# Half-products in both ConvGLUs of a two-layer decoder step, and one fixed place per feature tile for the modulation's matmuls

## The chip, the core and the metric

The kernel runs on one core of one Trainium2 chip, in one launch. The metric is the device time of the run in microseconds (us). Matmuls run on TensorE (PE; its weight loads are PEld), elementwise work on VectorE (DVE), ScalarE (ACT) and GpSimd (POOL); loads are issued by SyncE (SP), one queue, in order.

## What is computed

The program is one inference step of a two-layer decoder over 1024 prompt tokens and 8 sample tokens (1032 together, D_MODEL 1024, D_FF 2816). Layer 0 mixes tokens with a gated MLP, layer 1 with sparse attention; after each comes a ConvGLU:

```python
def ada_params(c, w_ada, b_ada):
    return (jax.nn.silu(c) @ w_ada + b_ada).reshape(c.shape[0], N_MOD, D_MODEL)

def conv_glu(h, w_up, conv_w, conv_b, w_down, past):
    a, u = jnp.split(h @ w_up, 2, axis=-1)
    t = a.shape[1]
    full = jnp.concatenate([past, a], axis=1)
    conv = sum(full[:, j:j + t] * conv_w[j] for j in range(CONV_W)) + conv_b
    y = (jax.nn.gelu(conv) * u) @ w_down
    return y, full[:, -(CONV_W - 1):]
```

`ada_params` gives the scales, shifts and gates (the modulation) of each layer. Those of layer 1 depend on `c` alone, so they can be computed at any time before layer 1.

## The kernel before

Everything lies with features on the partitions and tokens along the free axis. Float32 operands are split into a high and a low part, and each product is three matmuls: high by high, high by low, low by high (`mm3`, L97 is the one line of all such matmuls). Tokens come in chunks of 384, 384 and 264.

`conv_glu(l, ...)` walks over 22 feature tiles of 128. An **ordinary tile** (`parts`, `dense`) computes the gate and the up projection: 2 projections x 3 chunks x 8 blocks of the contraction x 3 = 144 matmuls into the four PSUM banks psA. Then it convolves, applies gelu and multiplies (DVE, ACT), and splits the result into `gh` and `gl`. The **down projection** of a tile (`down`) is 24 pieces of 3 matmuls into the four banks psB, each added to the residual R by DVE (`accumulate`, L649 and L653); these 72 matmuls wait in a queue `dq` and are dealt out between the matmuls of the next tile (`dpump`).

In the second ConvGLU only (`SEVEN = (1,)`) the tiles 4 to 21 are made by `seven_tile`. It takes gate and up weights as two halves of the contraction each (A11, A12 of the gate, A21, A22 of up) and the first 688 tokens as two chunks of 344 (`TH`), and forms that 2 x 2 block product from seven half-products, with sums of weights (S1 to S4, made by `sums` on POOL) and sums of inputs (F, made once by `form_steps` on DVE, ACT and POOL during tiles 2 and 3). The last 344 tokens take four plain half-products. A half-product is 12 matmuls of 344 columns (L840), so a tile has 11 x 12 = 132 of them. Each weight operand goes through `operand`: ACT makes the high half, POOL the low half (`ws`). The matmuls of these tiles are pinned in program order; in all other places a scheduler decides the order on each engine.

Raw weights land in three buffers (`raws`, `rawmk`), shared by gate and up weights (`wraw`, or `load_w` in an ordinary tile), down weights (`load_rows`, L137), the input sums and the modulation's weights.

**The modulation's steps** (`ada_round`). Layer 1's modulation is three rounds of eight steps and an end (`fin`: copy, four transposes, additions), 27 items in the deque `slow`, worked off inside the first ConvGLU. A step loads two raw buffers of 512 KB and issues four matmuls of 512 columns (L258), each into its own 32 partitions of one psB bank that a round holds from its first step to its end. The function `background` is called after each of the six parts of a tile and takes an item at every fourth call:

```python
            if slow and not fq and tick[0] % 4 == 0:
                slow.popleft()()
```

Of the kernel before, what the change touches and what calls it, by code (L numbers as in the profile page):

```python
# [17 lines left out]
KT = 8  # L18
# [29 lines left out]

KEEP = (3, 3)

SEVEN = (1,)
TH = 344
S0 = 4

# [7 lines left out]
def hybrid_step(  # L62
# [7 lines left out]
    V, A, G, PE, SP = nc.vector, nc.scalar, nc.gpsimd, nc.tensor, nc.sync  # L70
# [15 lines left out]
    def bank(tag="A"):  # L86
        return psum.tile([128, 512], F32, name="ps" + tag, tag="ps" + tag)
# [3 lines left out]
    def pinned(i):  # L91

        if pin[0]:
            tc.keep_in_program_order(i)
# [63 lines left out]
    fq = deque()  # L158
# [45 lines left out]
    SCT = sm.tile([128, KT, 32], F32, name="SCT", tag="x1")  # L204
    V.memset(SCT, 0.0)
    b = bank("B")
# [39 lines left out]
    def ada_round(L, r, mk):  # L246

        st = {}

        def step(k):  # L250
            if k == 0:
                st["b"] = bank("B")
            rw = [mk(), mk()]
            for half in range(2):
                SP.dma_start(rw[half][:, :1024],
                             w_ada[L, k * 128:(k + 1) * 128, 2048 * r + 1024 * half:2048 * r + 1024 * half + 1024])
            for g in range(4):
                PE.matmul(st["b"][32 * g:32 * g + 32, :512], SCT[:, k, :], rw[g // 2][:, (g % 2) * 512:(g % 2 + 1) * 512],  # L258
                          start=(k == 0), stop=(k == KT - 1), skip_group_check=True)

        def fin():
            S = mk()
            A.activation(S[:, :512], st["b"], AF.Copy)
            b2 = bank("B")
            for j in range(4):
                tr(b2[:, j * 128:(j + 1) * 128], S[:, j * 128:(j + 1) * 128])
            bb = PAR[:, pBADA + L * 48 + 16 * r:pBADA + L * 48 + 16 * r + 16].rearrange("p (g j) -> p g j", j=4)
            mo = MOD[L][:, 16 * r:16 * r + 16, :].rearrange("p (g j) c -> p g j c", j=4)
            src = b2.rearrange("p (j g c) -> p g j c", j=4, g=4)
            for g in range(4):  # L270
                V.tensor_tensor(mo[:, g], src[:, g, :, 0:9], bb[:, g].unsqueeze(2).to_broadcast([128, 4, 9]), op=OP.add)

        out = [lambda k=k: step(k) for k in range(KT)]
        out.append(fin)
        return out

    def rawmk():
# [169 lines left out]
    b = bank("B")  # L447
# [103 lines left out]
    b = bank("B")  # L551
    left = deque(range(KT))
    for n, (i, c) in enumerate((i, c) for c in range(3) for i in range(2)):
        z_half(i, c, 0)
        for _ in range(1 if n < 4 else 2):
            k = left.popleft()
# [61 lines left out]
    for i in range(8, 16):  # L618
        m = i - 8
        U[m] = Tt("U", tag="PPTT"[m % 4])  # L620
        for c in range(3):
            b = dense(pieces[i], 128, c)
# [46 lines left out]
    def conv_glu(l, R, gate, tail_af, last, slow, prefetch=None):  # L669
        up = ffn_w_up[l]  # L670
        keep = KEEP[l]

        seven = l in SEVEN

# [31 lines left out]
        def dpump(n):  # L706
            for _ in range(n):
                if dq:
                    dq.popleft()()

        tick = [0]

        def background():
            pump(2)
            tick[0] += 1
            if slow and not fq and tick[0] % 4 == 0:
                slow.popleft()()

        class Tile:
# [83 lines left out]
        def wraw(ff, s):  # L803
            if ff < FT:
                t = raws.tile([128, SLOT], F32, name="raw", tag="raw")
                SP.dma_start(t[:, :1024].rearrange("p (k c) -> p k c", k=KT),
                             up[:, s * F + ff * 128:s * F + (ff + 1) * 128].rearrange("(k p) c -> p k c", p=128))
                raw_w[ff, s] = [t[:, 0:512], t[:, 512:1024]]
# [27 lines left out]
        def half_product(b, w, xs, first, last=True):  # L836
            for k in range(4):
                x = [x[k] for x in xs]
                for n, (i, j) in enumerate(((0, 0), (0, 1), (1, 0))):
                    pinned(PE.matmul(b[:, :TH], w[i][:, k, :], x[j], start=first and k == 0 and n == 0, stop=last and k == 3 and n == 2,  # L840
                                     skip_group_check=True))

        def seven_tile(ff):
# [8 lines left out]
            def x(i, j):  # L852
                return [[H[:, 4 * i + k, j * TH:(j + 1) * TH] for k in range(4)] for H in (Hh, Hl)]
# [4 lines left out]
            def W(name):  # L858
                return ops[ff, name]
# [13 lines left out]

            def step(n):
                dpump(n)
                background()


            ba = bank("A")
# [10 lines left out]
            A.activation(p5, bb[:, :TH], AF.Copy)  # L890
            step(DP[2])
            operand(ff, "S4")
            wraw(ff + 1, 0)

            bd = bank("A")
            half_product(bd, W("S2"), t(1), True)
# [7 lines left out]
            conv(0, TH, ba, 0)  # L904
            gelu(a)
            step(DP[4])
            half_product(be, W("A12"), x(1, 2), False)
            A.activation(Cc[:, 2 * TH:NPT], be[:, :nr], AF.Identity, scale=w2, bias=cb)
            V.scalar_tensor_tensor(Cc[:, NPT:T], be[:, nr:TH], w2, PSC[l][:, ff, :], op0=OP.mult, op1=OP.add)
# [83 lines left out]
        if seven:  # L993
            operand(S0, "A11")
            sums(S0, 1)
            operand(S0, "S1")
            operand(S0, "S2")
            operand(S0, "A12")
            sums(S0, 3)
            dpump(len(dq) - 24)  # L1000
            pin[0] = True
            for ff in range(S0, FT):
                seven_tile(ff)
            pin[0] = False
# [15 lines left out]
        b = bank("B")  # L1020
# [11 lines left out]
    slow = deque(x for r in range(3) for x in ada_round(1, r, rawmk))  # L1032
# [61 lines left out]
    b = bank("B")  # L1094
# [323 lines left out]
    for w in range(2):  # L1418
        kf = [Tt("kf0", tag="P"), Tt("kf1", tag="P")]
        for kvh in range(2):  # L1420
# [4 lines left out]
            for c in range(3):  # L1425
                b = dense(pcs[i], 128, c)
# [334 lines left out]
```

## Time and profile before

| | |
|---|---|
| median of 3 runs | 2605.18 us (2605.16 to 2605.95) |
| the profiled execution's own time | 2597.94 us |
| its span, from the first instruction to the last | 2596.2 us |
| granted TensorE clock over the span | 0.985 |

| engine | busy us | share of the span |
|---|---|---|
| PE | 2495.1 | 96% |
| PEld | 2332.8 | 90% |
| DVE | 1679.4 | 65% |
| POOL | 1193.8 | 46% |
| ACT | 890.7 | 34% |

How to read it: the profile is one execution, and its times are us from the start of the span. A matmul's duration in a row reaches from its start to its modelled end and overlaps the next one; what a matmul costs PE in a stream is the distance from its start to the next start. The granted clock is given as a share of full speed. In the chain that ended last, a piece "PE x24" is 24 matmuls with nothing between them.

### The profile page before, as it was taken

To read this page: it belongs to the slowest core of one execution; us is meant where nothing else is said; L and a number is where in the kernel's file an instruction comes from. 1 tells how busy PE (TensorE), PEld (TensorE's weight loads), DVE (VectorE), ACT (ScalarE), POOL (GpSimd) and SP (SyncE) were. 2 spreads that over 40 slices of the span, in tenths; PEclk is the share of its full clock that TensorE was granted. 3 is DMA by queue.
4 is the path that set the end of the run, shared out by engine and by line. 5 is a ranking of instruction groups with operands and counts; after the bars stand their busy time and mean duration, and the time that the engine had idled before them with its cause. 6 is when DMAs were issued, how large, how long until landed. Compare 5 with 4: busy or idle time off the path is not lost.

```text
span 2596.2 us, 40912 instructions
## 1 busy us (share of the span) xinstructions
PE 2495.1 (96%) x15768; PEld 2332.8 (90%) x15768; DVE 1679.4 (65%) x3761; ACT 890.7 (34%) x1763; POOL 1193.8 (46%) x1236
## 2 busy tenths in 40 slices
PE   7999999999999999999998989898999999999996
PEld 5898899999999999998987988877999999999996
DVE  5233335667666666655687996533698788778777
ACT  4121234111111111113566876542523333333341
POOL 3332535223222322334435666533645666666665
PEclk9999999999999999999999999999999999999998
DMA  8414302322222223111113111133211111111111
GB/s 277 131 53 124 105 17 76 95 89 66 90 84 72 90 66 98 58 38 51 61 35 106 50 54 61 46 119 114 74 50 35 52 53 50 49 49 49 50 49 76
DMA packets 203977, 192.14 MB, mean 74 GB/s; under 512 B 9806, under 2 KB 178246, under 8 KB 202999
## 3 DMA queue, kind: packets, MB, share of 16 engines
q1 hardware_dynamic: 200582, 179.86, 22.2%
q0 software_dynamic: 2688, 9.44, 1.1%
q8 instruction: 125, 2.05, 0.3%
q14 instruction: 69, 0.57, 0.1%
q10 hardware_dynamic: 513, 0.23, 0.0%
HBM read 178.41 MB, written 11.27 MB: 73 GB/s over the span
## 4 chain that ended last, share of the span: by engine, by line
PE 83%; DVE 8%; POOL 3%; issue 2%; DMA 2%; ACT 2%; POOLq 0%; SPq 0%; DVEq 0%; ACTq 0%
PE psA L97 36%; PE psB L97 25%; PE psA L840 14%; PE psB L198 3%; PE psB L258 3%; DVE junk L1215 1%; DVE S L1195 1%; PE psA L198 1%; ACT junk L1246 1%; POOL whi L116 1%; DMA raw<-in_dsa_w_out_dram 0%; ACT Hh L384 0%; DMA adaw<-in_w_ada_dram 0%; DVE wh L119 0%; PE psA L1574 0%
## 5 line engine op out<-in xcount | busy, mean ns | idle before, releaser
L649 DVE SCALAR_TENSOR_TENSOR R<-psB,g,R 128x384 f32<-128x384 f32 (+1 forms) x976 | 537.0, 568 | 310.5 <-PE psB L97 308.1
L97 PE MATMUL psA<-Hh,whi 128*128 128x384 f32 (+1 forms) x2032 | 657.0, 324 | 12.5 <-POOL whi L116 7.9
L97 PE MATMUL psA<-Hl,whi 128*128 128x384 f32 (+1 forms) x2032 | 652.2, 322 | 1.0 <-POOL Hl L390 0.9
L97 PE MATMUL psA<-Hh,wlo 128*128 128x384 f32 (+1 forms) x2032 | 651.6, 321 | 1.4 <-DVE wlo L119 0.7
L116 POOL TENSOR_SCALAR whi<-raw 128x1024 fp32r<-128x1024 f32 (+1 forms) x125 | 137.3, 1098 | 653.6 <-PE psA L97 498.6
L97 PEld LDWEIGHTS psA<-Hh,whi 128*128 128x128 f32 x2032 | 382.9, 189 | 47.5 <-issue 28.2
L97 PEld LDWEIGHTS psA<-Hl,whi 128*128 128x128 f32 x2032 | 383.4, 189 | 9.3 <-issue 6.9
L97 PEld LDWEIGHTS psA<-Hh,wlo 128*128 128x128 f32 x2032 | 382.8, 188 | 8.2 <-issue 5.0
L97 PE MATMUL psB<-gh,whi 128*128 128x384 f32 (+1 forms) x1056 | 342.8, 325 | 5.9 <-DVE R L649 3.7
L119 POOL TENSOR_TENSOR wlo<-raw,whi 128x1024 fp32r<-128x1024 f32 (+1 forms) x127 | 319.4, 2516 | 47.1 <-ACT gh L114 25.5
L97 PE MATMUL psB<-gl,whi 128*128 128x384 f32 (+1 forms) x1056 | 338.7, 321 | 0.0
L97 PE MATMUL psB<-gh,wlo 128*128 128x384 f32 (+1 forms) x1056 | 338.2, 321 | 0.0
L840 PE MATMUL psA<-Hh,ws 128*128 128x344 f32 x1152 | 288.2, 320 | 0.0
L97 PEld LDWEIGHTS psB<-gh,whi 128*128 128x128 f32 x1056 | 199.2, 189 | 27.3 <-DVE R L649 11.2
L840 PEld LDWEIGHTS psA<-Hh,ws 128*128 128x128 f32 x1152 | 201.7, 188 | 0.0
L97 PEld LDWEIGHTS psB<-gl,whi 128*128 128x128 f32 x1056 | 199.4, 189 | 0.0
L97 PEld LDWEIGHTS psB<-gh,wlo 128*128 128x128 f32 x1056 | 199.1, 189 | 0.0
L840 PE MATMUL psA<-Hl,ws 128*128 128x344 f32 x576 | 183.8, 319 | 0.0
L114 ACT ACTIVATE gh<-Cc 128x384 fp32r<-128x384 f32 (+1 forms) x132 | 64.6, 490 | 301.8 <-DVE Cc L748 249.7
L119 DVE TENSOR_TENSOR gl<-Cc,gh 128x384 fp32r<-128x384 f32 (+1 forms) x132 | 159.3, 1209 | 13.1 <-ACT gh L114 12.2
L741 DVE SCALAR_TENSOR_TENSOR Cc<-As,PAR,Cc 128x383 f32<-128x383 f32 (+3 forms) x156 | 133.1, 856 | 23.1 <-ACT Cc L736 22.4
L97 PE MATMUL psB<-Hh,wh 128*128 128x384 f32 (+1 forms) x512 | 137.9, 341 | 9.3 <-DVE wh L119 6.6
(416 smaller groups left out, 4357.8 us busy)
## 6 DMA issues: line engine op xcount, KB each, us to landing
raw<-in_ffn_w_up_dram SPq DMA_DIRECT2D x88, 512.0 KB
raw<-in_w_ada_dram SPq DMA_DIRECT2D x64, 512.0 KB
raw<-in_ffn_w_down_dram SPq DMA_DIRECT2D x44, 512.0 KB
adaw<-in_w_ada_dram SPq DMA_DIRECT2D x32, 512.0 KB
raw<-in_sgu_w_in_dram SPq DMA_DIRECT2D x16, 512.0 KB
raw<-in_dsa_w_in_dram SPq DMA_DIRECT2D x16, 512.0 KB
raw<-in_dsa_w_out_dram SPq DMA_DIRECT2D x32, 256.0 KB
raw<-in_sgu_w_out_dram SPq DMA_DIRECT2D x8, 512.0 KB
```

Source lines behind the costliest of these rows:

```text
L97: pinned(PE.matmul(out, l, r, start=start, stop=stop))
L114: A.activation(hi, src, AF.Copy)
L116: G.tensor_scalar(hi, src, 1.0, 0.0, op0=OP.mult, op1=OP.add)
L119: (V if e_lo == "V" else G).tensor_tensor(lo, src, f(hi), op=OP.subtract)
L198: PE.transpose(out, in_, ident[:in_.shape[0], :in_.shape[0]])
L258: PE.matmul(st["b"][32 * g:32 * g + 32, :512], SCT[:, k, :], rw[g // 2][:, (g % 2) * 512:(g % 2 + 1) * 512], start=(k == 0), stop=(k == KT ...
L649: V.scalar_tensor_tensor(R[c][:, dt, :npr], b[:, :npr], gp[:, dt:dt + 1], R[c][:, dt, :npr], op0=OP.mult, op1=OP.add)
L741: V.scalar_tensor_tensor(Cc[:, a0:c0 + npr], As[:, a0 - d:c0 + npr - d], w, Cc[:, a0:c0 + npr], op0=OP.mult, op1=OP.add)
L840: pinned(PE.matmul(b[:, :TH], w[i][:, k, :], x[j], start=first and k == 0 and n == 0, stop=last and k == 3 and n == 2, skip_group_check=True))
L1195: V.scalar_tensor_tensor(S(b)[:, s:s + n], rl[:, :n], WI[:, b, h:h + 1], S(b)[:, s:s + n], op0=OP.mult, op1=OP.add)
L1215: V.tensor_scalar(junkV[:n, :W], x, c if c == 0.0 else f(c[:n, i:i + 1]), 0.0, op0=OP.is_ge, op1=OP.add, accum_out=cnt[:n, i:i + 1])
L1246: A.activation(junkA[:n, :W], x, AF.Sign, bias=c if c == 0.0 else f(c[:n, i:i + 1]), scale=scale if scale == -1.0 else scale[:n, i:i + 1], ...
```

## The change

1. `SEVEN = (0, 1)`: the tiles 4 to 21 of the first ConvGLU are made by `seven_tile` too, with its weight sums, operands and input forms.
2. `ada_round`'s step is cut in two, `load` and `times`. In a tile of half-products, `load` stands behind the operand S4, and `times` behind the fifth half-product and its share of down pieces; one item of `slow` per tile. Its matmuls are pinned as the others.
3. In the ordinary tiles 0 to 3 of the first ConvGLU an item is taken at every second call of `background` instead of every fourth. `background` is no longer called inside `seven_tile`.
4. The load of the next tile's gate weights, `wraw(ff + 1, 0)`, stands behind `times` instead of behind S4.

```diff
--- before.py
+++ after.py
@@ -48,7 +48,7 @@
 
 KEEP = (3, 3)
 
-SEVEN = (1,)
+SEVEN = (0, 1)
 TH = 344
 S0 = 4
 
@@ -247,16 +247,25 @@
 
         st = {}
 
-        def step(k):
-            if k == 0:
-                st["b"] = bank("B")
+        def load(k):
             rw = [mk(), mk()]
             for half in range(2):
                 SP.dma_start(rw[half][:, :1024],
                              w_ada[L, k * 128:(k + 1) * 128, 2048 * r + 1024 * half:2048 * r + 1024 * half + 1024])
+            return rw
+
+        def times(k, rw):
+            if k == 0:
+                st["b"] = bank("B")
             for g in range(4):
-                PE.matmul(st["b"][32 * g:32 * g + 32, :512], SCT[:, k, :], rw[g // 2][:, (g % 2) * 512:(g % 2 + 1) * 512],
-                          start=(k == 0), stop=(k == KT - 1), skip_group_check=True)
+                pinned(PE.matmul(st["b"][32 * g:32 * g + 32, :512], SCT[:, k, :], rw[g // 2][:, (g % 2) * 512:(g % 2 + 1) * 512],
+                                 start=(k == 0), stop=(k == KT - 1), skip_group_check=True))
+
+        def step(k, later=False):
+            rw = load(k)
+            if later:
+                return lambda: times(k, rw)
+            times(k, rw)
 
         def fin():
             S = mk()
@@ -270,8 +279,8 @@
             for g in range(4):
                 V.tensor_tensor(mo[:, g], src[:, g, :, 0:9], bb[:, g].unsqueeze(2).to_broadcast([128, 4, 9]), op=OP.add)
 
-        out = [lambda k=k: step(k) for k in range(KT)]
-        out.append(fin)
+        out = [lambda later=False, k=k: step(k, later) for k in range(KT)]
+        out.append(lambda later=False: fin())
         return out
 
     def rawmk():
@@ -713,7 +722,7 @@
         def background():
             pump(2)
             tick[0] += 1
-            if slow and not fq and tick[0] % 4 == 0:
+            if slow and not fq and tick[0] % (2 if seven else 4) == 0:
                 slow.popleft()()
 
         class Tile:
@@ -873,7 +882,6 @@
 
             def step(n):
                 dpump(n)
-                background()
 
 
             ba = bank("A")
@@ -890,7 +898,7 @@
             A.activation(p5, bb[:, :TH], AF.Copy)
             step(DP[2])
             operand(ff, "S4")
-            wraw(ff + 1, 0)
+            times = slow.popleft()(True) if slow else None
 
             bd = bank("A")
             half_product(bd, W("S2"), t(1), True)
@@ -904,6 +912,9 @@
             conv(0, TH, ba, 0)
             gelu(a)
             step(DP[4])
+            if times:
+                times()
+            wraw(ff + 1, 0)
             half_product(be, W("A12"), x(1, 2), False)
             A.activation(Cc[:, 2 * TH:NPT], be[:, :nr], AF.Identity, scale=w2, bias=cb)
             V.scalar_tensor_tensor(Cc[:, NPT:T], be[:, nr:TH], w2, PSC[l][:, ff, :], op0=OP.mult, op1=OP.add)
@@ -998,6 +1009,7 @@
             operand(S0, "A12")
             sums(S0, 3)
             dpump(len(dq) - 24)
+            tick[0] = 0
             pin[0] = True
             for ff in range(S0, FT):
                 seven_tile(ff)
```

What stands on the engines follows. On **PE**, in an ordinary tile of the first ConvGLU before: `raw,SCT` is the modulation's step, `psB<-g` a down piece, `psA<-H` the tile's projections.

```order
L97 MATMUL psA<-Hl,whi 128x264
L97 MATMUL psA<-Hh,wlo 128x264
L258 MATMUL psB<-raw,SCT 32x512
L97 MATMUL psB<-gh,whi 128x384
L97 MATMUL psB<-gl,whi 128x384
L97 MATMUL psB<-gh,wlo 128x384
L258 MATMUL psB<-raw,SCT 32x512 x3
L97 MATMUL psA<-Hh,whi 128x384
```

On PE in a tile of half-products of the first ConvGLU now (the half-product's line is L849, the step's L261):

```order
L97 MATMUL psB<-gh,whi 128x384
L97 MATMUL psB<-gl,whi 128x384
L97 MATMUL psB<-gh,wlo 128x384
L261 MATMUL psB<-raw,SCT 32x512 x4
L849 MATMUL psA<-Hh,ws 128x344
L849 MATMUL psA<-Hl,ws 128x344
L849 MATMUL psA<-Hh,ws 128x344 x2
```

A step's four matmuls stood in two pieces in most places; in these tiles they stand in one. In the whole first ConvGLU the 24 steps stood in 46 pieces before and stand in 33 now: 17 pieces for the eight steps that fall among the ordinary tiles, one piece for a step just ahead of tile 4, and 15 in the tiles. Two of the pieces among the ordinary tiles, as they stand now:

```order
L97 MATMUL psA<-Hh,wlo 128x384
L261 MATMUL psB<-raw,SCT 32x512
L97 MATMUL psB<-gh,whi 128x264
L97 MATMUL psB<-gl,whi 128x264
L97 MATMUL psB<-gh,wlo 128x264
L261 MATMUL psB<-raw,SCT 32x512
L97 MATMUL psA<-Hh,whi 128x384
```

There the scheduler still cuts a step, here into single matmuls around one down piece.

On **SP** in the middle of the first ConvGLU before (L255 the modulation's loads, L125 gate or up weights, L137 down weights):

```order
L255 DMA raw<-in_w_ada_dram 128x1024 x2
L125 DMA raw<-in_ffn_w_up_dram 128x8x128
L137 DMA raw<-in_ffn_w_down_dram 128x1024
L125 DMA raw<-in_ffn_w_up_dram 128x8x128
L255 DMA raw<-in_w_ada_dram 128x1024 x2
```

and now, one tile and the next (L253 the modulation's loads, L815 gate and up weights):

```order
L815 DMA raw<-in_ffn_w_up_dram 128x8x128 x2
L137 DMA raw<-in_ffn_w_down_dram 128x1024
L253 DMA raw<-in_w_ada_dram 128x1024 x2
L815 DMA raw<-in_ffn_w_up_dram 128x8x128 x2
L137 DMA raw<-in_ffn_w_down_dram 128x1024
```

Each tile has five loads in a fixed sequence: the step's two, then the next tile's gate and up weights, then the down weights. In the second ConvGLU nothing moves on any engine: the scheduler put the gate weights' load at the same place as before. All rows of PE up to the end of the first ConvGLU's tile 0 (2470) and from the middle of layer 1's projections on (7405) are the same in both programs.

## Rows read from the trace of the kernel before

**Rows 1.** The page: span, PE's share, and PE in 40 slices.
```profile
span 2596.2 us, 40912 instructions
...
PE 2495.1 (96%) x15768; PEld 2332.8 (90%) x15768; DVE 1679.4 (65%) x3761; ACT 890.7 (34%) x1763; POOL 1193.8 (46%) x1236
...
PE   7999999999999999999998989898999999999996
```

**Rows 2.** Stretches: us, busy (and count) PE, PEld, DVE, ACT, POOL; clock, DMA share, GB/s.
```profile
613.73:835.86 222.13, 222.13 (x1365) 206.43 (x1365) 144.02 (x288) 36.69 (x80) 63.25 (x36) 1.00 0.26 81
2003.53:2453.18 449.65, 449.65 (x2858) 449.65 (x2857) 361.30 (x743) 156.44 (x294) 289.66 (x210) 1.00 0.16 50
```

**Rows 3.** The chain that ended last: start, length, piece (384, 264, 344 columns).
```profile
1090.89 4.22 PE psA L97 x24
1097.21 2.92 PE psA L97 x24
...
2035.73 5.65 PE psA L840 x36
```

**Rows 4.** Timeline of PE around a whole step (876.80) and half a split one.
```profile
876.59 0.28 PE L97 MATMUL psA<-Hh,wlo 128*128 128x264 f32 x1
876.80 1.06 PE L258 MATMUL psB<-raw,SCT 128*32 128x512 f32 x8
...
878.02 0.28 PE L97 MATMUL psA<-Hl,whi 128*128 128x264 f32 x1
...
1023.33 0.33 PE L97 MATMUL psB<-gh,wlo 128*128 128x384 f32 x1
1023.59 1.04 PE L258 MATMUL psB<-raw,SCT 128*32 128x512 f32 x2
...
1024.79 0.34 PE L97 MATMUL psB<-gh,whi 128*128 128x384 f32 x1
```

**Rows 5.** PE's waits, second ConvGLU's ordinary tiles (1875 to 1975): us, times, longest.
```profile
PE psB L97 <- DVE R L649: 3.5, 5, 1.4
PE psA L97 <- ACT Cc L736: 0.6, 1, 0.6
```

**Rows 6.** Timeline of SP and POOL, one tile of half-products, second ConvGLU.
```profile
2102.56 4.67 SPq L806 DMA_DIRECT2D raw<-in_ffn_w_up_dram  x2
2120.41 0.34 SPq L137 DMA_DIRECT2D raw<-in_ffn_w_down_dram  x1
...
2099.92 2.61 POOL L119 TENSOR_TENSOR wlo<-raw,whi 128x1024 fp32r<-128x1024 f32 x1 [1.58 <-ACT gh L114]
2102.50 1.56 POOL L821 TENSOR_TENSOR sf<-raw 128x512 f32<-128x512 f32 x1
...
2105.55 1.29 POOL L119 TENSOR_TENSOR ws<-raw,ws 128x512 fp32r<-128x512 f32 x1
...
2111.29 1.30 POOL L818 TENSOR_TENSOR sf<-raw 128x512 f32<-128x512 f32 x1 [0.41 <-DMA raw<-in_ffn_w_up_dram]
...
2132.02 2.60 POOL L119 TENSOR_TENSOR wlo<-raw,whi 128x1024 fp32r<-128x1024 f32 x1 [1.59 <-ACT gh L114]
```

**Rows 7.** Timeline of ACT, DVE and PE, the end of the same tile.
```profile
2124.88 0.63 ACT L114 ACTIVATE ws<-sf 128x512 fp32r<-128x512 f32 x1 [2.79 <-PE psA L840]
2125.42 0.66 ACT L925 ACTIVATE Cc<-X,PAR 128x344 f32<-128x344 f32 x1
...
2132.68 2.32 DVE L119 TENSOR_TENSOR gl<-Cc,gh 128x344 fp32r<-128x344 f32 x1
...
2135.47 1.07 DVE L119 TENSOR_TENSOR gl<-Cc,gh 128x344 fp32r<-128x344 f32 x1
...
2131.85 0.32 PE L840 MATMUL psA<-Hh,ws 128*128 128x344 f32 x1
...
2137.51 0.34 PE L97 MATMUL psB<-gh,whi 128*128 128x384 f32 x1
```

**Rows 8.** Stretch at the end of the first ConvGLU, columns as in the second group.
```profile
1180.00:1215.00 35.00, 32.63 (x230) 31.80 (x229) 22.73 (x65) 13.81 (x22) 11.12 (x18) 0.98 0.01 3
```

## The prediction

> **What bounds the kernel now.** I read the page first: PE is busy 96% of the span, and in the slices that hold the two ConvGLUs it stands at nine tenths or more [rows 1]. A busy PE is not yet PE at its peak, so the second view is the stretches: six tiles of the first ConvGLU take 222.13 us, fourteen tiles of half-products in the second take 449.65, PE busy in all of it at the full granted clock (2.4 GHz), DVE at most 80%, POOL 64%, the DMA engines 26% [rows 2]. The third is the chain, which gives what a matmul costs in a stream: 4.22 / 24 = 0.176 us for 384 columns, 2.92 / 24 = 0.122 for 264, 5.65 / 36 = 0.157 for 344 [rows 3]. With these prices both stretches close. An ordinary tile's projections are 96 x 0.176 + 48 x 0.122 = 22.74 us, a tile's down pieces 48 x 0.176 + 24 x 0.122 = 11.37, so six tiles are 204.7; the other 17.5 us belong to the modulation's steps. Fourteen tiles of half-products are 14 x (132 x 0.157 + 11.37) = 449.3 of 449.65. So in both stretches the order of PE's own matmuls is the time, and no other engine is waited for. That makes the sum one of matmuls, with a check on whether the other engines still keep up.
>
> **The change part by part.**
>
> *Half-products in the tiles 4 to 21 of the first ConvGLU.* Removed per tile: 22.74 us. Added: 132 x 0.157 = 20.72. The gain is 2.02 us a tile, over 18 tiles **36.4 us**. It is all on the path, since PE has no gap there [rows 2]. The Trainium skill (TensorE: Matmul & The Clock Gate, Back-to-back issue gap) gives a warm matmul its columns at 2.4 GHz plus 2.5 ns. By that a tile would gain 1.75 us and the 18 tiles 31.5, some 5 us less; this case's rows show 14 ns instead of 2.5 above the columns' time, at all three widths, and I keep to the rows.
>
> *The modulation's steps in fewer pieces.* A whole step of four matmuls (eight records) pushes the next matmuls from 876.59 to 878.02: 1.43 us, of which two matmuls of 264 columns are 0.244, so a piece costs 1.19. A piece of one matmul (two records) takes 1023.33 to 1024.79, 1.46 less 0.298, or 1.16 [rows 4]. A piece costs the same whether it holds one matmul or four, since the four write different partitions and run beside one another. I take 1.17. (The 15 pieces among the six tiles make 17.6 us: the 17.5 left over above.) From 46 pieces to 33 is 13 x 1.17 = **15.2 us** gained. The 24 steps and three ends are otherwise the same work.
>
> *Input forms in the ordinary tiles 2 and 3, and twice as many steps among the tiles 0 to 3.* The first ConvGLU gets what the second has: DVE makes the input sums while it also owes R its down pieces. In the second ConvGLU PE waited there 3.5 us for R and 0.6 for Cc [rows 5]. That is the nearest row; I take the whole **4.1 us** as a loss. Bounds: 0, since the steps give DVE more time per tile here and the sums are dealt out more evenly; and twice that, 8.2, since a step's round holds one of the four psB banks, so that three are left for down pieces.
>
> *The new loads of each tile.* Here the tile of the second ConvGLU serves as the clock. Its last half-product starts at 2131.85, so the next tile begins at 2131.85 + 12 x 0.157 = 2133.7 and this one began 449.65 / 14 = 32.12 earlier, at 2101.6 [rows 2, 7]. `times` stands behind 60 half-product matmuls and 27 of down pieces: 9.4 + 4.3 later, at 2115.3. The step's first load goes into the buffer that the down weights leave, at 2099.92 + 2.61 = 2102.5; its second into the one that the gate weights leave, behind A12's low half, 2105.55 + 1.29 = 2106.8. At these very instants SP issues its two loads now (2102.56, the second ending at 2107.23), and the second is there when POOL goes on at 2111.29, 4.1 us after its issue [rows 6]. So the step's data are there 4.0 us early: **no wait**.
>
> *The gate and up weights behind the step.* They can start only when the step has been read, 2115.3 + 1.2 = 2116.5, instead of 2102.56. One load takes 0.34 to issue and 4.1 more, 4.4; two take between 4.4 and 8.9. Then POOL sums them (2 x 1.30) and ACT makes S1's high half and after it Cc: between 2123.5 and 2128.0, against 2124.88 plus the step's 1.17, 2126.05, in the tile's own pace [rows 6, 7]. At worst that is 1.95 us late. What follows is DVE's `gl`, which ends at 2135.47 + 1.07 = 2136.54, and PE wants it at 2137.51: 0.97 us to spare [rows 7]. So a tile loses between 0 and 1.0 us. With the DMA engines idle three quarters of the time [rows 2] two loads overlap; I take 0. A11's low half comes behind the sums on POOL, by 2130 at worst, and the next tile begins at 2133.7 + 1.2.
>
> *The end of the layer.* The same down pieces, norms and projections follow in nearly the same order. PE stands idle there for 2.4 of 35 us [rows 8]; bounds -2.4 and +2.4, taken as 0. The second ConvGLU's order is unchanged: 0.
>
> **Sum:** -36.4 - 15.2 + 4.1 = -47.5. The profiled execution took 2597.94, so 2550.4; the median of the runs shown stands 7.2 above it, so **2557.7 us**. The unknown costs alone make 2551 to 2564.
>
> **The rivals.**
>
> *The weights behind the step come late.* Each of the 15 tiles with a step loses the 1.0 us above: 15 us, 2572.7. For it: the margin at the tile's end is only 0.97 us. Against: it needs two loads to run strictly one after the other.
>
> *DVE falls behind POOL.* Of two equal `gl` operations in one tile one takes 2.32 us and one 1.07, and POOL's 2.60 us for the down weights ran from 2132.02 to 2134.62, across the long one [rows 6, 7]. If in the first ConvGLU POOL falls on the second one too, it ends 1.25 later, 0.28 past the margin: 5 us over 18 tiles, and with the forms' upper bound (4.1 more) 2566.9. The Trainium skill (SBUF — State Buffer, SBUF: two separate sides) has it as a rule that speaks against giving both engines more work: a GpSimd operation and a DVE operation with two SBUF inputs exclude each other for a whole instruction. The trace agrees with 2.32 against 1.07. Against it as a loss: the second ConvGLU pays the same, and its 14 tiles close without it.
>
> *Slower: the loads close a loop.* One tile's step waits for a buffer that POOL frees; POOL waits for the up weights; these wait for the step before. The loop is 4.4 (up weights), 2.6 (sums), 3.9 (three low halves), 2.6 (down weights), 3.1 (two sums), 1.3 (A12), 4.4 (the step's second load), 1.2 (the step): 23.5 us, against 33.3 of a tile [rows 6]. It decides when it exceeds 33.3, and eats the whole gain at 33.3 + 47.5 / 15 = 36.5, that is, if each of the loads took 11 us instead of 4.4. With loads of 13.3 us it would be 41.3, 8.0 a tile: 2678.
>
> *No change.* The loop exceeds the tile by some 3 us, and gains and losses cancel: about 2605. That the change does not do what it says I rule out: the order on PE shows the 132 matmuls and the unsplit steps.
>
> **How the numbers follow.** The forecast 0.78, late weights 0.10, DVE behind 0.07, no change 0.02, the loop 0.03. The range goes from the forecast's low end, less 3 us because executions of one kernel differ by up to 7.2 here, to the late weights with 2 us on top: 2548 to 2575. About 0.2% (5.2 us) is what a measurement of this kernel can tell from no change; every case but the last two is faster by more. So faster 0.95, within it 0.02, slower 0.03.
>
> **What would show it.** In the changed profile: chain pieces of 36 and 12 matmuls at 0.157 in the first ConvGLU; a tile with a step every 33.3 us, one without every 32.1; step pieces of eight records; PE busy throughout. A wait of PE for DVE's `gl` or R at a tile's first down pieces would show the first or second rival, a wait for the modulation's raw load the loop. Among the tiles 0 to 3, PE's wait for R between 0 and 8 us. I am wrong if the tiles' period exceeds 34 us, or the tiles 0 to 3 lose over 10.

## The result, and the profile after

The changed kernel takes **2571.04 us** (median of 4 runs, 2568.10 to 2572.03); the kernel before, in the same comparison, 2605.43 (2605.16 to 2605.95). The ratio is 0.9866 (95% interval 0.9849 to 0.9883), a gain of 34.4 us where 47.5 were forecast. The direction was right and the time lies in the range, 13.3 us above the forecast.

The changed kernel's page, to be read against [rows 1]: PE's share is the same 96%, with 33 us less of busy time.

```profile
span 2568.7 us, 41113 instructions
...
PE 2461.7 (96%) x15552; PEld 2307.6 (90%) x15552; DVE 1749.2 (68%) x3927; ACT 990.7 (39%) x1915; POOL 1386.0 (54%) x1406
...
PE   7999999999999999999989989898999999999996
```

The first ConvGLU, from its first down piece to the transposes behind its last, is one stretch before and four after (columns as in the stretches of [rows 2]). Before:

```profile
436.07:1210.21 774.14, 774.14 (x4809) 726.68 (x4805) 491.77 (x976) 139.72 (x298) 229.49 (x141) 1.00 0.24 74
```

After: the ordinary tiles 0 to 3, the entry of tile 4, the other tiles of half-products, and the down pieces behind the last tile. The last lines are two stretches about the start of tile 4 and one tile with a step (from step to step).

```profile
438.91:553.56 114.65, 113.42 (x673) 93.84 (x669) 89.72 (x187) 23.34 (x48) 39.62 (x27) 1.00 0.36 111
553.56:580.00 26.44, 23.41 (x135) 22.00 (x134) 19.79 (x35) 9.47 (x19) 13.49 (x10) 0.94 0.29 85
580.00:1134.98 554.98, 553.76 (x3526) 536.85 (x3525) 426.63 (x874) 193.09 (x364) 353.46 (x257) 1.00 0.25 75
1134.98:1176.20 41.22, 39.60 (x265) 38.71 (x264) 25.47 (x51) 13.87 (x23) 16.60 (x19) 1.00 0.05 13
...
548.00:560.00 12.00, 12.00 (x82) 12.00 (x81) 12.00 (x19) 5.69 (x12) 7.74 (x5) 1.00 0.01 1
564.00:569.00 5.00, 4.99 (x21) 4.99 (x22) 2.37 (x5) 1.26 (x2) 3.65 (x4) 0.66 0.41 114
672.55:705.82 33.27, 33.27 (x213) 32.19 (x212) 25.31 (x54) 11.26 (x21) 20.68 (x15) 1.00 0.26 80
```

Before, PE was busy in all of 774.14 us. After, the stretch takes 737.29, that is 36.85 less, and PE has gaps: the sum of the busy times is 730.18. The tile's period is 33.27, against 33.3 forecast. What is lost lies in few places. The waits of PE there (430 to 1180: us in total, times, longest):

```profile
PE psB L97 <- DVE R L658: 3.8, 4, 3.0
PE psB L97 <- POOL wlo L119: 1.4, 1, 1.4
PE psA L198 <- ACT R L401: 1.1, 2, 0.9
PE psB L97 <- DVE t L662: 1.1, 2, 0.5
PE psA L97 <- ACT Cc L745: 0.6, 1, 0.6
```

Worked out from the starts of every 132nd half-product, the 18 tiles take, in us (the end of a round, which has no step, falls in the tile marked e; in the last row, of the experiment with both repairs and two more, tile 4 has no step either; the last two tiles have fewer down pieces):

```
tile             4     5     6     7     8     9     10    11    12    13    14    15    16    17    18    19    20    21
changed          38.23 33.29 33.22 33.31 33.25 33.31 33.21 32.53e 34.21 33.65 33.25 34.24 33.62 33.29 33.22 33.27 21.35e 21.15
again            38.21 33.29 33.22 33.31 33.25 33.30 33.22 32.52e 34.46 33.66 33.25 34.38 33.60 33.29 33.22 33.27 21.35e 20.96
both and two     32.18 33.29 33.22 33.27 33.25 33.31 33.21 33.28 33.22 32.51e 33.25 33.30 33.21 33.29 33.22 33.27 21.97 26.40
```

**Tile 4 loses 4.9 us.** DVE is busy in every one of the 12 us from 548 to 560, PE then waits 3.0 us for R, and in the 5 us behind that wait the granted clock is 0.66 of full speed (between the levels of 1.2 and 2.4 GHz). What went before, on SP, POOL, DVE and PE:

```profile
533.53 2.68 SPq L253 DMA_DIRECT2D raw<-in_w_ada_dram  x2
543.79 0.38 SPq L815 DMA_DIRECT2D raw<-in_ffn_w_up_dram  x1
...
542.70 1.07 PE L261 MATMUL psB<-raw,SCT 128*32 128x512 f32 x8
...
547.58 1.68 POOL L827 TENSOR_TENSOR raw<-raw 128x512 f32<-128x512 f32 x1 [21.56 <-DMA raw<-in_ffn_w_up_dram]
549.34 1.36 POOL L828 TENSOR_TENSOR raw<-raw 128x512 f32<-128x512 f32 x1
550.66 1.56 POOL L119 TENSOR_TENSOR ws<-raw,ws 128x512 fp32r<-128x512 f32 x1
...
546.97 1.14 DVE L750 SCALAR_TENSOR_TENSOR Cc<-As,PAR,Cc 128x384 f32<-128x384 f32 x2
...
551.00 1.64 DVE L750 SCALAR_TENSOR_TENSOR Cc<-As,PAR,Cc 128x384 f32<-128x384 f32 x1
...
564.01 0.44 PE L97 MATMUL psB<-gh,whi 128*128 128x384 f32 x1 [3.03 <-DVE R L658]
```

The step just ahead of tile 4 (its loads at 533.53) has a raw buffer that tile 4's up weights wait for; PE comes to the step at 542.70, and the load goes out behind it, at 543.79 only. POOL, which sat idle for 21.56 us until they landed, begins its sums at 547.58, and from there DVE's operations beside them get long: 1.64 us for the same convolution that takes 0.57 (1.14 for two) just before.

**The tiles 12, 13, 15 and 16 lose 2.6 us together**, against 33.29. It begins with late weights. For the next tile's up weights POOL waits 2.60 us in tile 12, and 0.97 in tile 13:

```profile
846.41 1.30 POOL L827 TENSOR_TENSOR sf<-raw 128x512 f32<-128x512 f32 x1 [2.60 <-DMA raw<-in_ffn_w_up_dram]
...
879.39 1.30 POOL L827 TENSOR_TENSOR sf<-raw 128x512 f32<-128x512 f32 x1 [0.97 <-DMA raw<-in_ffn_w_up_dram]
```

So POOL's low halves fall on DVE's work at the end of tile 12. Two equal DVE convolutions there (851.04) and at the end of tile 13 (885.27), and POOL beside the first pair:

```profile
851.04 3.21 DVE L874 SCALAR_TENSOR_TENSOR Cc<-X,PAR,Cc 128x344 f32<-128x344 f32 x2
...
885.27 1.18 DVE L874 SCALAR_TENSOR_TENSOR Cc<-X,PAR,Cc 128x344 f32<-128x344 f32 x2
...
851.06 2.81 POOL L119 TENSOR_TENSOR ws<-sf,ws 128x512 fp32r<-128x512 f32 x2
```

The pair takes 3.21 us beside POOL's 2.81 and 1.18 where POOL is out of the way. PE then waits for DVE's `t` (854.86, in tile 12) and for `gl` at the first down pieces of tile 13 (862.29). The tiles 15 and 16 repeat it, with a wait of 2.59 us for the weights and a pair of 3.21 us at 952.16. The Trainium skill (SBUF — State Buffer, SBUF: two separate sides) has it that of a GpSimd operation and a DVE operation with two SBUF inputs the one that starts first holds the shared ports for its whole length. The trace agrees: 3.21 is 1.18 plus 2.03, most of POOL's 2.81.

The late weights come first in the other profiles too. In seven of them (both of this kernel, and those of the experiments 5, 6 and 7) the tiles 5 to 19 lose where POOL waits 2.06 us or more for these weights, or in the tile behind, and more the longer it waits: some 0.6 us after 2.2, 0.9 after 2.6, 1.6 after 3.2. Where it waits up to 1.95 us, they lose nothing (a tile with an end of a round and a step aside). What makes these loads late is not shown. While the one of tile 12 is under way (839.2 to 847), the trace has one packet of the queue that loads instructions, and so it has in tile 15 (940.3 to 948); in the tiles 13 and 14 it has none (873.8 to 881, 907 to 914), and in two others that lose nothing it comes at the end of the load (645.3 and 745.0):

```profile
q8 instruction: 1, 0.02, 1.0%
```

### The profile page after: what moved, and what is told of

The parts are those of the page before. It is cut to its first block, busy times and chain, and to the rows that moved or that the text cites. A ratio compares the mean times of both kernels' runs of the same rounds, so it can differ in the third digit from the quotient of the medians.

```text
span 2568.7 us, 41113 instructions
## 1 busy us (share of the span) xinstructions
PE 2461.7 (96%) x15552; PEld 2307.6 (90%) x15552; DVE 1749.2 (68%) x3927; ACT 990.7 (39%) x1915; POOL 1386.0 (54%) x1406
## 5 line engine op out<-in xcount | busy, mean ns | idle before, releaser
L849 PE MATMUL psA<-Hh,ws 128*128 128x344 f32 x2304 | 577.9, 320 | 0.0
L849 PEld LDWEIGHTS psA<-Hh,ws 128*128 128x128 f32 x2304 | 403.6, 188 | 12.6 <-issue 12.6
L97 PE MATMUL psA<-Hh,whi 128*128 128x384 f32 (+1 forms) x1168 | 381.2, 328 | 13.0 <-POOL whi L116 7.8
L97 PE MATMUL psA<-Hh,wlo 128*128 128x384 f32 (+1 forms) x1168 | 378.8, 325 | 0.6 <-DVE wlo L119 0.5
L97 PE MATMUL psA<-Hl,whi 128*128 128x384 f32 (+1 forms) x1168 | 378.6, 325 | 0.5 <-POOL Hl L399 0.5
L849 PE MATMUL psA<-Hl,ws 128*128 128x344 f32 x1152 | 367.7, 319 | 0.0
L119 POOL TENSOR_TENSOR ws<-raw,ws 128x512 fp32r<-128x512 f32 x152 | 201.5, 1327 | 238.8 <-ACT ws L114 238.8
L849 PE MATMUL psA<-F,ws 128*128 128x344 f32 x1296 | 222.5, 321 | 0.0
L97 PEld LDWEIGHTS psB<-gh,whi 128*128 128x128 f32 x1056 | 199.4, 189 | 20.3 <-DVE R L658 12.5
L849 PEld LDWEIGHTS psA<-Hl,ws 128*128 128x128 f32 x1152 | 216.2, 188 | 0.0
L849 PEld LDWEIGHTS psA<-F,ws 128*128 128x128 f32 x1296 | 208.2, 189 | 0.2 <-issue 0.2
```

Of the source, the lines that this page charges most:

```text
L97: pinned(PE.matmul(out, l, r, start=start, stop=stop))
L119: (V if e_lo == "V" else G).tensor_tensor(lo, src, f(hi), op=OP.subtract)
```

## The experiments

Each ratio is to the kernel before, in the same comparison, with its 95% interval. What a kernel does in the first ConvGLU is read from its profile, against 774.14 us before and 737.29 after.

**1. The two kernels once more.** No edit.

> The kernel before, unchanged, looked at once more. The attention stage (from the first kc transpose to the last) took 407.4 us in the first profile and 397 to 408 in five other kernels whose order of instructions there is the same. Theory (executions differ there by themselves): this profile shows another value there, by several us, at another granted clock, and the rest within 2 us. Rival (a kernel's value is its own): 407 again, and the difference between two kernels there belongs to the kernels.

> The changed kernel, unchanged. Theory (the ConvGLUs repeat, the start and the attention stage do not): the first ConvGLU takes 737.3 us again within 0.3, the waits of PE at 564.01 (3.0 us for R) and at the two tiles (0.5 us for t) come back; the rest of the span differs by several us. Rival: the wait at tile 4 is a chance of one execution, and this one has 732 us there.

The kernel before, first profile and second (the start, the first ConvGLU, the attention stage):

```profile
0.00:436.07 436.07, 413.39 (x2658) 367.72 (x2658) 162.80 (x398) 121.11 (x215) 173.59 (x187) 0.99 0.35 111
...
1376.69:1784.08 407.39, 375.64 (x2388) 329.68 (x2389) 270.99 (x736) 249.02 (x523) 221.14 (x399) 0.95 0.25 77
```

```profile
0.00:443.20 443.20, 422.04 (x2657) 375.35 (x2657) 162.86 (x398) 121.30 (x215) 172.68 (x187) 0.96 0.35 109
443.20:1217.34 774.14, 774.14 (x4808) 726.63 (x4805) 489.58 (x976) 139.97 (x298) 229.73 (x141) 1.00 0.24 74
1383.20:1793.40 410.20, 375.67 (x2388) 327.18 (x2389) 270.69 (x736) 249.16 (x523) 220.95 (x399) 0.96 0.25 76
```

The first expectation holds in part. The spans are 2596.2 and 2613.0. The first ConvGLU takes 774.14 us in both, to the hundredth; the start takes 7.1 us more at a lower granted clock (0.96 for 0.99), the attention stage 2.8 more; so "the rest within 2 us" is true of the ConvGLUs alone (some 7 us more lie between them, outside the attention stage). The changed kernel, again: 2569.28 us (0.9855, 0.9836 to 0.9873), its first ConvGLU 737.49, the same waits at the same places. So that stage can be compared between two profiles to some tenths of a us, and the rest of the span cannot, below some 10 us. One premise of the first expectation does not hold: PE's order in the attention stage (from the last QI product on) is not the same in all kernels. The kernel before, the changed one and those of the experiments 3 and 4 share it, and take 405.3 to 410.2 us there in six profiles. In the other six kernels the scheduler orders it otherwise, and they take 397.3 to 402.1. So the totals of the experiments 2, 5, 6 and 7 hold some 8 us of gain that has nothing to do with what was to be tested. What follows is therefore judged by the first ConvGLU's time, and the totals are given beside it.

**2. Half-products alone.** The kernel before with one line changed:

```diff
-SEVEN = (1,)
+SEVEN = (0, 1)
```

> The kernel before with nothing but the half-products in the first ConvGLU's tiles 4 to 21; the steps come at every fourth call, unpinned, where the kernel before had them. Its order on PE has 36 pieces of steps in the first ConvGLU, the changed kernel 33, the kernel before 46. Theory 1 (the time is PE's own order): -36.4 - 10 x 1.17 + up to 5 of waits for R at the front: 2605.4 - 45 = 2560 to 2566, that is, the fixed place gives next to nothing beyond three pieces. Rival (the fixed place is what keeps the steps' loads off the path): steps at changing places make PE wait for a raw load or for late weights, several us in many tiles, and the run takes 2580 or more.

Measured: **2657.73 us**, ratio 1.0196 (1.0182 to 1.0210), slower than before by 51 us. The theory fell by far, the rival held. The waits of PE in its first ConvGLU, its tiles of half-products up to the last step and behind it, and one step on PE and its loads on SP:

```profile
PE psB L258 <- DMA raw<-in_w_ada_dram: 57.8, 23, 4.5
```

```profile
546.39:920.00 373.61, 314.88 (x1720) 264.39 (x1718) 195.44 (x417) 89.25 (x165) 159.72 (x118) 0.91 0.29 86
920.00:1233.11 313.11, 311.67 (x1976) 311.39 (x1977) 243.19 (x496) 113.11 (x214) 202.86 (x148) 0.99 0.17 51
```

```profile
642.31 1.05 PE L258 MATMUL psB<-raw,SCT 128*32 128x512 f32 x4 [3.82 <-DMA raw<-in_w_ada_dram]
...
631.15 7.73 SPq L255 DMA_DIRECT2D raw<-in_w_ada_dram  x2
```

The steps themselves are not pinned here, but the half-products and down pieces around them are, and a step stands close behind the call that loads it; its second load is issued at 638.5 (631.15 + 7.73, less the 0.33 of one issue), and PE stands 3.82 us until it has landed. 23 such waits make 57.8 us. The granted clock is 0.91 until the last step: at most about 0.09 x 373.6 = 34 us, since PE also waits in part of the slow time. The 12 pieces more than in the changed kernel's tiles (27 for 15) make 14. Together that is up to 106, against the 105.3 us by which these tiles take longer than the changed kernel's (686.72 for 581.42); as those hold 7.5 us of losses of their own, some 7 us are not placed. So what the parts 2 to 4 of the change are worth to the half-products is 86.7 us, 2657.7 less 2571.0, and in the first ConvGLU alone 98.0, 835.30 less 737.29. These parts change three things at once: the distance between load and use, the place, and the number of steps in a tile (19 in the tiles 4 to 11 here, one a tile in the change). Experiment 3 takes back the distance alone; the other two are not told apart.

**3. Load and use at one place.** The changed kernel, with

```diff
-            times = slow.popleft()(True) if slow else None
+            if slow:
+                slow.popleft()()
...
-            if times:
-                times()
```

> The changed kernel with a step's loads and its four matmuls both at the place of the loads, behind S4: still one fixed place per tile, still pinned, but nothing between load and use. On PE the step then stands two half-products and 15 down matmuls earlier: 24 x 0.157 + 15 x 0.158 = 6.1 us. In the changed kernel the second load of a step is issued at 663.56 and the step starts at 672.55, 9.0 us later; a load takes 0.34 + 4.1, so its data are there 4.6 us early. Theory (it is the distance between load and use that the fixed place buys): PE waits 6.1 - 4.6 = 1.5 us per step for the raw load, 15 times, 22 us, with a fallen clock on top: 2593 to 2605. Rival (the fixed place itself, or pinning, is what counts): 2571 within 5.

Measured: 2591.85 us, ratio 0.9940 (0.9924 to 0.9956); the first ConvGLU 757.57, that is 20.3 us over the changed kernel. The theory holds, though the time is 1 us under its range: the place is as fixed and as pinned as in the change, and half of the gain is gone. A step of this kernel, and one of the changed kernel:

```profile
641.12 2.06 PE L261 MATMUL psB<-raw,SCT 128*32 128x512 f32 x8
```

```profile
672.55 1.06 PE L261 MATMUL psB<-raw,SCT 128*32 128x512 f32 x8
```

The step lasts 1.0 us longer, since its second half waits inside it; a steady tile takes 34.3 to 34.4 us instead of 33.2 to 33.3. So a step waits 1.05 us, not 1.5: its data come 5.0 us ahead of the changed kernel's step (the forecast had 4.0). The tiles with a step behind tile 4 lose 12.6 us together (the four that were late in the changed kernel take 34.3 to 34.4 as well), and tile 4 loses 7.7, 45.90 instead of 38.23.

**4. Whole steps without half-products.** The kernel before, with

```diff
-            for g in range(4):
-                PE.matmul(st["b"][32 * g:32 * g + 32, :512], ...)
+            for g in (2, 3, 0, 1):
+                i = PE.matmul(st["b"][32 * g:32 * g + 32, :512], ...)
+                tc.keep_in_program_order(i)
```

> The kernel before, without half-products in the first ConvGLU; only the four matmuls of a step are pinned in order, those of the second load first. 24 pieces in the first ConvGLU instead of 46, 8 instead of 15 ahead of it. Theory: 1.17 us a piece, 22 x 1.17 = 25.7 us in the first ConvGLU and 0 to 8.2 ahead of it: 2605.4 - 25.7 = 2580, down to 2571. Rival: the scheduler had split the steps to cover their loads, so whole steps make PE wait for raw loads as in the half-products alone (57.6 us there): no gain or a loss, 2600 or more.

Measured: 2577.90 us, ratio 0.9882 (0.9867 to 0.9897). The first ConvGLU, which took 774.14:

```profile
434.30:1182.79 748.49, 748.49 (x4809) 724.08 (x4806) 498.27 (x976) 139.98 (x298) 229.97 (x141) 1.00 0.24 76
```

It is 25.65 us shorter (25.7 expected), 1.166 us for each of the 22 pieces, with no wait of PE. In the total this edit alone brings nearly nine tenths of what the whole change brings (1.18% for 1.34%), in the first ConvGLU seven tenths (25.65 us for 36.85).

**5. The changed kernel with every step whole.** The same edit as in 4, in the changed kernel.

> The four matmuls of each step are pinned in order in every place, those of the second load first, so that a step is one piece everywhere: 24 pieces in the first ConvGLU instead of 33, and 8 instead of 15 in the stages before it. Theory 1: a piece costs 1.17 us whatever it holds, so the first ConvGLU gains 9 x 1.17 = 10.5 us, nearly all of it in the tiles 0 to 3; the stages before gain 0 to 8.2 us, as far as PE sets their time. 2571.0 - 10.5 = 2560.5, down to 2552. Rival: the pinned step now makes PE wait for the second load, which the split had covered; then PE waits for the modulation's raw load appear among the tiles 0 to 3 and the gain is under 5 us (2566 or more).

Measured: 2552.92 us, ratio 0.9785 (0.9772 to 0.9799); the first ConvGLU 730.30, 7.0 us less than in the changed kernel. The ordinary tiles:

```profile
433.22:540.01 106.79, 103.61 (x673) 92.84 (x670) 85.90 (x187) 23.26 (x48) 40.31 (x27) 1.00 0.38 119
```

They take 106.79 us for 114.65, 7.9 less, where nine pieces at 1.17 make 10.5: with less to do, PE waits more for DVE there (1.7 us for R and 1.1 for `t`, against 1.1 and none, counted as what the distance from one matmul's start to the next exceeds the price of its kind). The rival's wait for a second load is 0.35 us, once. So the theory holds for the piece, and about a quarter of it comes back as waits. The total gains 18, more than this stage explains. The stages ahead of it, with 7 pieces fewer, end at 433.22, for 438.91 and 441.90 in the changed kernel's two profiles; behind it, the reordered attention stage takes 401.1 us for 408.5.

**6. No step just ahead of tile 4.** The changed kernel, with

```diff
-            if slow and not fq and tick[0] % (2 if seven else 4) == 0:
+            if slow and len(slow) > 18 and not fq and tick[0] % (2 if seven else 4) == 0:
```

> The step just ahead of tile 4 (542.70 in the changed kernel's trace) is left for a later tile: the step count in the tiles goes from 15 to 16, nothing is left out. Theory 1: that step holds a raw buffer, tile 4's up weights land late, POOL's sums then fall on DVE's down pieces, and tile 4 loses 5.0 us (PE's wait of 3.2 us for R at 560.64 and a granted clock of 0.66 behind it). Then both are gone, the stretch 553 to 580 is 5 us shorter and the run takes 2571.0 - 5 = 2566. Rival: DVE is late at tile 4 anyway, because it makes the input forms among down pieces; the wait of about 3 us stays and the time stays within 1.5 us of 2571.

Measured: 2559.27 us, ratio 0.9815 (0.9802 to 0.9829). By the total this is more than the theory asked for, but the first ConvGLU takes 737.15 us, the same as in the changed kernel: the gain of 12 lies in other stages, 11 of it in the reordered attention stage (397.3 us for 408.5), and proves nothing here. In the stage, the same stretch of tile 4 and the waits of PE:

```profile
556.38:582.82 26.44, 25.32 (x152) 23.32 (x151) 14.77 (x31) 7.93 (x16) 17.56 (x13) 1.00 0.33 100
```

```profile
PE psB L97 <- DVE R L658: 1.3, 4, 0.5
...
PE psB L261 <- DMA raw<-in_w_ada_dram: 1.1, 1, 1.1
```

The long wait for R is gone (longest 0.5), the clock is 1.00 for 0.94, 152 matmuls stand where 135 stood, and DVE is busy 14.77 for 19.79. That is the mechanism of the theory. But tile 4 still takes 35.51 us, since now its own step waits 1.1 for its load: 2.7 gained, not 5. The moved step and the last end, which now falls among the down pieces behind the last tile (43.70 us for 41.22), take it back. The cause is shown, the repair is none.

**7. Both repairs, and further ones.** First 5 and 6 together:

> Both edits together: no step just ahead of tile 4, and every step whole. If the two losses are separate, the gains add: 2571.0 - 5 - 10.5 = 2555.5, down to 2547 with the stages ahead of the first ConvGLU. If the wait at tile 4 is DVE's own (rival of the first), 2560; if whole steps make PE wait (rival of the second), 2566 or more.

Measured: **2540.51 us**, ratio 0.9740 (0.9725 to 0.9754); the first ConvGLU 727.36, 9.9 us under the changed kernel, where the two expected gains add up to 15.5. Tile 4's step waits 2.1 us for its load. The next kernel takes that step away too and loads tile 20's down weights earlier:

```diff
-            times = slow.popleft()(True) if slow else None
+            times = slow.popleft()(True) if slow and ff > S0 else None
...
             wraw(ff + 1, 0)
+            if ff == FT - 1:
+                wload(ff - 1, 2)
```

> Both repairs, and two more: tile 4 takes no step (with both repairs its step made PE wait 2.13 us for the raw load at 558.90), so the last item, an end of a round, falls behind the last tile; and the down weights of tile 20 are loaded earlier in tile 21, so that POOL has their low half sooner (PE waited 1.69 us for it at 1128.80). If both waits go and the moved end is hidden: 2540.5 - 3.8 = 2537; if the moved end costs what it did without these (tail of 43.7 instead of 41.2 us): 2539; if POOL is held there by its wait for the next stage's loads, not by the order of the down weights, the second wait stays and it is 2539 to 2541.

Measured: 2545.50 us, ratio 0.9762 (0.9749 to 0.9775), above the 2537 to 2541 expected, though the first ConvGLU has 724.88, the shortest of all. Both waits are gone, and tile 4 takes 32.18 us (the table above), a tile without a step and without a loss. In their place tile 21's step waits:

```profile
1096.54 1.06 PE L261 MATMUL psB<-raw,SCT 128*32 128x512 f32 x8 [2.82 <-DMA raw<-in_w_ada_dram]
```

The last one puts the sixteen steps into the tiles 5 to 20, by taking an end and the next step in one tile:

```diff
+            if slow and ff > S0 and not times:
+                times = slow.popleft()(True)
```

> Both repairs and the two further edits, with one more: the end of the second round is taken in the same tile as the first step of the third, so that the sixteen steps stand in the tiles 5 to 20 and the tiles 4 and 21 have none. With the two further edits alone, tile 21's step made PE wait 2.82 us for its second load (1096.54), whose buffer POOL frees late there. Theory: this wait goes, the first ConvGLU takes 724.9 - 2.8 = 722 us. Rival: the end and a step in one tile take one raw buffer more, the next weights come late by it, and the first ConvGLU stays at 724 or more.

Measured: 2543.13 us, ratio 0.9755 (0.9741 to 0.9770); the first ConvGLU 726.50. Its tiles and what follows them:

```profile
538.78:1114.48 575.70, 575.47 (x3667) 557.34 (x3666) 435.41 (x900) 201.32 (x377) 366.39 (x267) 1.00 0.26 78
1114.48:1157.90 43.42, 41.48 (x265) 40.26 (x265) 25.66 (x51) 13.84 (x23) 16.86 (x19) 0.96 0.05 13
```

The tiles are the best of all: PE is busy in 575.47 of 575.70 us (in the changed kernel 577.17 of 581.42). But POOL's order changed behind them, the wait for the down weights' low half came back (1.63 us), and the clock fell with it. So the theory holds for tile 21's wait and not for the stage, whose time is the rival's (724 or more), by another wait than the rival named. By the ratios the three cannot be told apart with certainty; the two edits of 5 and 6 are the simplest of them, and all beat both kernels by 1% or more, of which the reordered attention stage (399.1 to 402.1 us) gives 5 to 9 us.

## Why the prediction was right or wrong

**What bounds the kernel: right.** Where PE has no gap the order of its own matmuls is the time, and the stage repeats to the hundredth.

**Half-products, -36.4: right in size, on a condition that the sum did not price.** An ordinary tile's matmuls are 34.11 us by [rows 3], a tile of half-products without a step takes 32.18 (experiment 7, tile 4) or 32.12 [rows 2]; 18 times 1.93 to 1.99 is 34.7 to 35.8. The formula of the Trainium skill (TensorE: Matmul & The Clock Gate, Back-to-back issue gap), which that section gives for an isolated matmul and not for a stream of weight loads and matmuls, had given 31.5. The runs decide for the rows: a half-product's matmul costs the same 0.157 us in the first ConvGLU as in the second. Only the 14 ns that the prediction has above the columns' time at all three widths are rounded too far: by [rows 3] they are 12, 14 and 16 at 264, 344 and 384 columns. The condition is that no step makes PE wait. The prediction took the fixed place for a saving in pieces, and its "no wait" for the loads for a cost left out. Experiment 2 shows that without the parts 2 to 4 of the change the half-products make the kernel 51 us slower than before.

**Pieces, 13 x 1.17 = -15.2: right.** Experiment 4 gives 1.166 each.

**The ordinary tiles, +4.1 (0 to 8.2): right within its bounds.** PE waits 1.9 us there, 1.1 for R and the rest for Cc, counted as in experiment 5.

**Step's data 4.0 us early, no wait: right**, and a little cautious: 5.0 (experiment 3).

**Weights behind the step, 0 to 1.0 a tile, taken as 0: right** in ten of the fifteen tiles with a step, whose period is what was forecast (33.2 to 33.3). In the tiles 12 and 15 it exceeds 34 us, the prediction's own sign of being wrong, and PE's wait for `gl` at the next tile's first down pieces is the sign that it had named for the rivals.

**What failed is the entry into the tiles of half-products, which the sum took as free, and with it the 0 for late weights.** The sum is -35.3 (the middle) - 15.2 = -50.5, and the stage gained 36.85: 13.7 us were lost where 4.1 were allowed for. The prediction priced the ordinary tiles by the second ConvGLU and the tiles of half-products by their steady state, and took the entry between them as free. There the second ConvGLU has no step; the first has one just ahead, whose loads hold a raw buffer that tile 4's up weights need. So 4.9 us went there: the rival of late weights, in one tile, by way of the rival of DVE beside POOL, whose price per event (1.25 us forecast, 2.03 measured as 3.21 less 1.18) was in the text. 2.6 went in the tiles 12, 13, 15 and 16 in the same way, late weights first and DVE beside POOL by them, 0.3 to 1.0 us each where the term had 0. Why the weights are late just there stays open: with the end of the round one or two tiles later (experiment 7) these tiles keep their pace, and in two of the three kernels there the tiles 18 or 19 lose 0.3 to 0.6 instead, behind a wait of POOL of 2.1 or 2.2 us. Tile 4's cause is shown by an experiment, that of these four tiles by the traces alone. 2.0 went behind the last tile (POOL's low half above all, where the term for the end of the layer had 0) and 1.9 in the ordinary tiles. That is 11.4 of 13.7; the rest are delays too short to be placed.

**The profile's 7.2 us below the median.** It stands outside the first ConvGLU, as experiment 1 shows. Carrying it over to the forecast was right: the medians differ by 34.4 where the stage gained 36.85, and the 2.5 between lie within what the other stages do by themselves.

So the miss of 13.3 us is 10.7 in the first ConvGLU (47.5 less 36.85), 2.5 in stages that the change does not touch, and 0.2 by which the kernel before itself took longer in the comparison (2605.43 for 2605.18).

**The range and the rivals.** The range held the time by 4 us, and that is in part luck: its upper end stands for 1.0 us lost to late weights in each of 15 tiles, and they cost 4.9 us in one tile, 2.6 in four and nothing in ten. The loop was never near: no tile of the steady state exceeded 33.3 us by more than 1.2. It is its neighbour that was missing among the rivals for the other side: a place at which load and use stand too close, which costs 20.3 us where nothing else is altered (experiment 3), and 57.8 us of waits where several steps crowd into a tile as well (experiment 2).

## What to carry to other kernels

A pinned order takes from a scheduler the freedom that hid a load: whoever pins work around a load must put the distance between load and use back by hand, and check it as time from the last issue to the use, since 6 us less of it cost half of this change. Price the seam between two regimes by itself, with the buffers that the last piece of the one still holds when the first of the other wants them; the steady state says nothing of it. And judge an experiment by the stage that it edits: experiment 6 won 12 us in total, nearly all by another order of a stage that it does not name, and nothing in the stage of its theory.

## What the runs showed of the hardware

- A stage in which PE never waits repeats to 0.01 us (774.14 twice), on two executions whose totals differ by 16.8 us. The differences lie in stages in which PE waits at times and the granted clock falls: 0.99 and 0.96 at the start of the same program.
- Four 32-column matmuls that write different partitions cost PE one piece of 1.166 us, as two of them or one do; splitting them paid nothing, and joining them gave 25.65 us, for the 36.85 that the seven-product scheme and its fixed place gave in this kernel.
- A single wait of PE of 3.0 us was followed by 5 us at a granted clock of 0.66; 23 waits of 0.2 to 4.5 us, spread over 374 us, by a mean of 0.91 there. The clock's share of that loss is at most 34 of 105 us, an estimate from these rows.
- Loads of one kind, issued at the same place of their tiles, kept POOL waiting 1.0 us in one tile and 2.6 in another (879.39 and 846.41); in the tiles 5 to 19 time was lost only at or behind a wait of 2.06 us or more.
